# Sharing one reciprocal and one weight product among four heads in a mixture-of-softmaxes kernel, with other exponential tiles, fewer waits and an order set by hand

## The chip, the cores and the metric

One core of one Trainium2 chip. Times are device microseconds (us) of whole executions. The profiled span is about 2 us shorter than the time (781.4 for 783.36 us). A run is called fast when it lies within 1.5% of the fastest of the same kernel; all comparisons here are between fast runs.

## The reference

Shapes: logits 32 x 128 x 4 x 4096 and prior 32 x 128 x 4, fp32; output 32 x 128 x 4096.

```python
prior_probs = np.exp(prior - prior.max(axis=-1, keepdims=True))
prior_probs = prior_probs / prior_probs.sum(axis=-1, keepdims=True)
softmax = np.exp(logits - logits.max(axis=-1, keepdims=True))
softmax = softmax / softmax.sum(axis=-1, keepdims=True)
mixture = np.sum(prior_probs[..., None] * softmax, axis=2)
```

Each of the 4096 rows has four heads of 4096 logits. The kernel takes exponentials without subtracting the maximum, sums them on the way, and adds the four heads, each times prior / sum. It reads 268.5 MB and writes 67.1 MB.

## The kernel before

The work is cut into 32 units of 128 rows. A unit's load is 8.39 MB (128 rows of 64 KB), its store 2.10 MB. Two load tiles alternate; exponentials are taken on ACT (ScalarE) and go to two tiles by turns; each head gets its own reciprocal on DVE (VectorE) and, except head 0, its own product on POOL (GpSimd). SP (SyncE) issues the loads. In the cut of the code that follows, the comments are mine.

```python
for b in range(B):
    ...
    if 0 < b < B - 3:
        store(b - 1, eng=nc.scalar)          # the store of the unit before, on ACT's queue
    for h in range(H):
        ...
        et = lt[:, h] if inplace else ebuf[:, h % 2]
        ex = nc.scalar.activation(et, lt[:, h], AF.Exp, accum_out=dsum[:, col])
        ...
        nc.vector.reciprocal(rden[:, col], dsum[:, col])
        if h == 0:
            nc.vector.tensor_scalar(out=acc, in0=et, scalar1=rden[:, col], scalar2=pp[...],
                                    op0=ALU.mult, op1=ALU.mult)
            continue
        nc.gpsimd.tensor_mul(coeff[:, col], rden[:, col], pp[...])
        ...
            nc.vector.scalar_tensor_tensor(out=acc[:, cs], in0=et[:, cs], scalar=coeff[:, col],
                                           in1=acc[:, cs], op0=ALU.mult, op1=ALU.add)
            if split:                         # the very last add and its store, in two halves
                store(b, c * w, (c + 1) * w)
    if b + 2 < B:
        load(b + 2)
    if b == B - 3:                            # the last stores go behind the loads, on SP's queue
        store(b - 1)
        store(b)
    elif b == B - 2:
        store(b)
```

Loads of unit 0 and of the last three units go in four pieces of one head each. The last two units work inside the load tile.

The softmax here doesn't subtract the row's maximum and nothing guards it: scores larger than these inputs give would overflow.

## Time and profile before

| | before |
|---|---|
| time, median of the first 3 runs | 783.39 us (783.36 to 783.53) |
| profiled span | 781.4 us |
| DVE, ACT, POOL busy | 531.3, 470.4, 19.3 us |
| bytes over the span | 335.67 MB, 430 GB/s |
| DMA queues together | 99.7% of 16 engines' span |

The page lists the busy time of each engine, then 40 slices of the span, then the DMA queues. In the chain of waits, columns are start, duration, and what the step is. In tables by stretches: the stretch, its length, busy us of DVE, ACT and POOL with counts, clock, DMA share, GB/s. The DMA share books each packet at one moment, so a short stretch can read a little over 1.00. The lines that carry the argument stand in the prediction.

### The profile page before, as it was taken

Reading aid. Unit: us, or ns where it says so; the run is one execution under the profiler, and the core shown is the slowest. Engines: PE = TensorE matmul, PEld = TensorE weight load, DVE = VectorE, ACT = ScalarE, POOL = GpSimd, SP = SyncE. Lnnn points to the kernel's source line nnn. Section 1 sums busy time; section 2 is a strip of 40 time slices with the busy share of each in tenths; the row PEclk is TensorE's granted clock in tenths of the full one; section 3 lists DMA queues with packets and bytes.
Section 4 is the critical chain, followed back from the end, with each engine's and each line's share of the span. In section 5 each row is a group of like instructions: output and inputs, shape, how many; then the busy total and the mean of one; then the engine's idle time right before and its main releaser. Section 6 shows DMA issues by size and latency. Waiting matters only on the chain.

```text
span 781.4 us, 853 instructions
## 1 busy us (share of the span) xinstructions
DVE 531.3 (68%) x266; ACT 470.4 (60%) x258; POOL 19.3 (2%) x101
## 2 busy tenths in 40 slices
DVE  6647678656786666866667765677666776668994
ACT  5366556755567555576555765457655577558971
POOL 0000000000000000000000000000000000000000
DMA  9999999999999999999999999999999999999998
GB/s 377 445 416 456 416 419 453 416 457 408 461 406 466 406 463 409 426 447 424 448 413 465 404 461 405 460 420 451 411 451 418 433 439 416 456 413 429 429 429 357
DMA packets 11127, 335.67 MB, mean 430 GB/s; under 512 B 1248, under 2 KB 1248, under 8 KB 1264
## 3 DMA queue, kind: packets, MB, share of 16 engines
q1 hardware_dynamic: 7056, 276.83, 82.1%
q10 hardware_dynamic: 4064, 58.79, 17.6%
q14 instruction: 7, 0.06, 0.0%
HBM read 268.50 MB, written 67.11 MB: 429 GB/s over the span
## 4 chain that ended last, share of the span: by engine, by line
DMA 66%; ACT 14%; DVE 10%; issue 7%; SPq 0%; POOL 0%; DVEq 0%; POOLq 0%; ACTq 0%
DMA ltile<-in_logits_dram 66%; ACT ebuf L110 14%; DVE acc L131 9%; DVE ltile L131 1%; SPq L51 0%; POOL coeff L126 0%; DVE rden L119 0%; DVEq L169 0%; DVE ltile L121 0%; POOLq L169 0%; ACTq L110 0%
## 5 line engine op out<-in xcount | busy, mean ns | idle before, releaser
L110 ACT ACTIVATE ebuf<-ltile 128x4096 f32<-128x4096 f32 x120 | 433.0, 3609 | 284.1 <-DMA ltile<-in_logits_dram 240.5
L131 DVE SCALAR_TENSOR_TENSOR acc<-ebuf,coeff,acc 128x4096 f32<-128x4096 f32 x90 | 403.6, 4484 | 27.3 <-POOL coeff L126 27.3
L119 DVE RECIPROCAL rden<-dsum 128x1 f32<-128x1 f32 x128 | 20.4, 159 | 203.8 <-ACT ebuf L110 203.8
L121 DVE TENSOR_SCALAR acc<-ebuf,rden,pp 128x4096 f32<-128x4096 f32 x30 | 72.4, 2412 | 1.1
L126 POOL TENSOR_TENSOR coeff<-rden,pp 128x1 f32<-128x1 f32 x96 | 18.2, 189 | 747.1 <-DVE rden L119 747.1
L110 ACT ACTIVATE ltile<-ltile 128x4096 f32<-128x4096 f32 x8 | 28.9, 3608 | 4.3 <-DMA ltile<-in_logits_dram 4.3
L131 DVE SCALAR_TENSOR_TENSOR ltile<-ltile,coeff 128x4096 f32<-128x4096 f32 (+1 forms) x7 | 27.0, 3874 | 1.8 <-POOL coeff L126 1.8
L110 ACT ACTIVATION_READ_ACCUMULATOR ebuf<-ltile 128x1 f32 x120 | 22.4, 187 | 0.0
L121 DVE TENSOR_SCALAR ltile<-ltile,rden,pp 128x4096 f32<-128x4096 f32 x2 | 4.8, 2414 | 0.1
L68 DVE TENSOR_REDUCE pmax<-pr 16x256 f32<-16x1024 f32 x1 | 1.2, 1207 | 4.8 <-DMA pr<-in_prior_dram 4.8
L70 ACT ACTIVATE pr<-pr 16x1024 f32<-16x1024 f32 x1 | 1.1, 1055 | 4.9 <-DVE pr L69 4.9
L70 ACT ACT_TABLE_LOAD x1 | 1.3, 1283 | 1.2 <-PEq L158 1.2
L73 DVE TENSOR_TENSOR pn<-pr,pmax 16x1024 f32<-16x1024 f32 x1 | 1.9, 1906 | 0.1
L71 DVE TENSOR_REDUCE pmax<-pr 16x256 f32<-16x1024 f32 x1 | 1.2, 1207 | 1.1 <-ACT pr L70 1.1
L80 DVE STREAM_TRANSPOSE pp<-pn 32x256 f32<-32x256 f32 x4 | 1.7, 434 | 0.1
L72 DVE RECIPROCAL pmax<-pmax 16x256 f32<-16x256 f32 x1 | 1.7, 1741 | 0.0
L110 ACT ACTIVATION_READ_ACCUMULATOR ltile<-ltile 128x1 f32 x8 | 1.5, 186 | 0.0
L69 DVE TENSOR_TENSOR pr<-pr,pmax 16x1024 f32<-16x1024 f32 x1 | 1.2, 1214 | 0.0
L66 POOL MEMSET pn<- 32x1024 f32 x1 | 0.9, 941 | 0.3 <-POOLq L158 0.3
L158 POOL MEMSET const-float32-0.0<- 128x1 f32 x1 | 0.1, 103 | 0.2 <-issue 0.2
L158 POOL MEMSET const-bfloat16-1.0<- 128x1 bf16 x1 | 0.1, 106 | 0.0
L158 POOL MEMSET const-uint8-127<- 128x1 uint8 x1 | 0.1, 106 | 0.0
(1 smaller groups left out, 0.1 us busy)
## 6 DMA issues: line engine op xcount, KB each, us to landing
out_dram<-acc ACTq DMA_DIRECT2D x28, 2048.0 KB, 29.3
ltile<-in_logits_dram SPq DMA_DIRECT2D x16, 2048.0 KB, 20.4
out_dram<-acc SPq DMA_DIRECT2D x2, 2048.0 KB, 32.9
out_dram<-ltile SPq DMA_DIRECT2D x1, 2048.0 KB, 21.2
out_dram<-ltile SPq DMA_DIRECT2D x2, 1024.0 KB, 8.7
ltile<-in_logits_dram SPq DMA_DIRECT2D x28, 32.3
pr<-in_prior_dram ACTq DMA_DIRECT2D x1, 64.0 KB, 4.1
```

The lines of the kernel that those rows point to most:

```text
L68: nc.vector.reduce_max(pmax, pr, axis=AX.X)
L69: nc.vector.tensor_sub(pr, pr, pmax.unsqueeze(2).to_broadcast([G, R, H]))
L70: nc.scalar.activation(pr, pr, AF.Exp)
L71: nc.vector.reduce_sum(pmax, pr, axis=AX.X)
L72: nc.vector.reciprocal(pmax, pmax)
L73: nc.vector.tensor_mul(pn[0:G].rearrange("g h r -> g r h"), pr, pmax.unsqueeze(2).to_broadcast([G, R, H]))
L80: nc.vector.transpose(pp[32 * t : 32 * (t + 1)], pq[:, :, :, 32 * t : 32 * (t + 1)])
L110: ex = nc.scalar.activation(et, lt[:, h], AF.Exp, accum_out=dsum[:, col])
L119: nc.vector.reciprocal(rden[:, col], dsum[:, col])
L121: nc.vector.tensor_scalar(out=acc, in0=et, scalar1=rden[:, col], scalar2=pp[:, b % J, h, b // J : b // J + 1], op0=ALU.mult, op1=ALU.mult,)
L126: nc.gpsimd.tensor_mul(coeff[:, col], rden[:, col], pp[:, b % J, h, b // J : b // J + 1])
L131: nc.vector.scalar_tensor_tensor(out=acc[:, cs], in0=et[:, cs], scalar=coeff[:, col], in1=acc[:, cs], op0=ALU.mult, op1=ALU.add,)
```

## The change

The intent: take work and waits from DVE, ACT and POOL. One reciprocal of four columns and one product of four columns serve all heads of a unit. Head 0's exponential is written over its own logits, heads 1 and 3 go to SBUF tiles, head 2 to PSUM, so that ACT need not wait for a tile that DVE still reads. Each instruction keeps only the waits named for it, and the order of the program is that of the source. In exchange the adds of a unit wait for its fourth exponential, the next load into the tile waits for the first add, and the store goes out later.

```diff
-            et = lt[:, h] if inplace else ebuf[:, h % 2]
-            ex = nc.scalar.activation(et, lt[:, h], AF.Exp, accum_out=dsum[:, col])
-            nc.vector.reciprocal(rden[:, col], dsum[:, col])
-            nc.gpsimd.tensor_mul(coeff[:, col], rden[:, col], pp[...])
+    ebuf1 = cpool.tile([P, V], FP32, name="ebuf1")
+    ebuf2 = psum.tile([P, V], FP32, name="ebuf2")
+    ebuf3 = cpool.tile([P, V], FP32, name="ebuf3")
+            byhead = u >= U - 3
+            es = (lt[:, 0], ebuf1, ebuf2, ebuf3) if bufd else [lt[:, h] for h in range(H)]
...
+            if not byhead:
+                for h in range(H - 1):
+                    exp(h)
+                if u:
+                    store(u - 1, obuf[:, (u - 1) % 2], nc.scalar)
+                exp(H - 1, ...)
+                mul = weigh(0, H, *free)      # one reciprocal, one product, 128x4
+                for h in range(H):
+                    add(h, mul)
+            else:                              # the last three units: head by head as before
+                for h in range(H):
+                    exp(h)
+                    mul = weigh(h, 1, ...)
+                    ...
...
+            if u >= 2:                         # in load(u)
+                only(ld, adds[u - 2, 0] if h == 0 else exps[u - 2, h])
```

(`only` keeps the waits that are named and drops the others; parts of the diff are left out, and the comments are mine.)

More of the change, by code (lines that the diff above doesn't have):

```diff
@@ L29 @@
     G = B * S // R
-    B = G * J
-    assert G * R == B * S and G <= 32
+    U = G * J
+    assert G * R == B * S and G <= 32 and H == 4
     lg = logits.rearrange("b s h v -> (b s) h v").rearrange("(g p j) h v -> g j p h v", p=P, j=J)
@@ L35 @@
     pv = prior.rearrange("b s h -> (b s) h").rearrange("(g r) h -> g r h", r=R)
-    lpool = ctx.enter_context(tc.tile_pool(name="lpool", bufs=2))
-    apool = ctx.enter_context(tc.tile_pool(name="apool", bufs=2))
     cpool = ctx.enter_context(tc.tile_pool(name="cpool", bufs=1))
-    def pieces(b):
-        return 1 if b == 0 or b >= B - 3 else H
-    ltiles = {}
-    def load(b, eng=nc.sync):
-        lt = lpool.tile([P, H, V], FP32, name="ltile")
-        n = pieces(b)
-        for h in range(0, H, n):
-            eng.dma_start(out=lt[:, h : h + n], in_=lg[b // J, b % J, :, h : h + n, :])
-        ltiles[b] = lt
@@ L54, with only @@
-    accs = {}
-    def store(b, lo=0, hi=V, eng=nc.sync):
-        eng.dma_start(out=ov[b // J, b % J, :, lo:hi], in_=accs[b][:, lo:hi])
-    load(0, eng=nc.sync)
+    psum = ctx.enter_context(tc.tile_pool(name="psum", bufs=1, space=bass.MemoryType.PSUM))
+    before = {}
+    def only(ins, *keep):
+        for k in keep:
+            tc.add_manual_dep(
+                ins.ins,
+                k.ins.name,
+                mybir.DependencyInfo(mybir.DependencyClass.Sync, mybir.DependencyReason.DATA),
+                reason="all that this instruction waits for",
+            )
+        tc.declare_no_dep(
+            ins.ins,
+            group="loop",
+            keep=[k.ins for k in keep] + before.get(ins.ins.engine, []),
+            reason="covered by the waits that are kept",
+        )
+        tc.add_to_no_dep_group("loop", ins.ins)
+        before[ins.ins.engine] = [ins.ins]
+        return ins
@@ new lines, with load @@
+    ltile = cpool.tile([P, 2, H, V], FP32, name="ltile")
+    loads = {}
+    exps = {}
+    adds = {}
+    stores = {}
+    def load(u):
+        n = 1 if u == 0 or u >= U - 3 else H
+        for h in range(0, H, n):
+            ld = nc.sync.dma_start(
+                out=ltile[:, u % 2, h : h + n], in_=lg[u // J, u % J, :, h : h + n, :]
+            )
+            if u >= 2:
+                only(ld, adds[u - 2, 0] if h == 0 else exps[u - 2, h])
+            else:
+                only(ld)
+            for k in range(h, h + n):
+                loads[u, k] = ld
@@ L62, with store @@
+    def store(u, acc, eng, lo=0, hi=V):
+        st = eng.dma_start(out=ov[u // J, u % J, :, lo:hi], in_=acc[:, lo:hi])
+        stores[u] = only(st, adds[u, H - 1])
     pr = cpool.tile([G, R, H], FP32, name="pr")
-    nc.scalar.dma_start(out=pr, in_=pv)
-    load(1, eng=nc.sync)
     pn = cpool.tile([32, H, R], FP32, name="pn")
-    nc.gpsimd.memset(pn, 0.0)
     pmax = cpool.tile([G, R], FP32, name="pmax")
-    nc.vector.reduce_max(pmax, pr, axis=AX.X)
-    nc.vector.tensor_sub(pr, pr, pmax.unsqueeze(2).to_broadcast([G, R, H]))
@@ L70 @@
-    nc.scalar.activation(pr, pr, AF.Exp)
-    nc.vector.reduce_sum(pmax, pr, axis=AX.X)
-    nc.vector.reciprocal(pmax, pmax)
-    nc.vector.tensor_mul(
-        pn[0:G].rearrange("g h r -> g r h"), pr, pmax.unsqueeze(2).to_broadcast([G, R, H])
-    )
-    pq = pn.rearrange("g h (p j) -> g j h p", j=J)
-    pp = cpool.tile([P, J, H, 32], FP32, name="pp")
-    for t in range(P // 32):
-        nc.vector.transpose(pp[32 * t : 32 * (t + 1)], pq[:, :, :, 32 * t : 32 * (t + 1)])
-    NCHUNK = 2
-    dsum = cpool.tile([P, B * H], FP32, name="dsum")
@@ L86 @@
-    rden = cpool.tile([P, B * H], FP32, name="rden")
-    coeff = cpool.tile([P, B * H], FP32, name="coeff")
-    ebuf = cpool.tile([P, 2, V], FP32, name="ebuf")
-    exps = []
-    for b in range(B):
-        last = b == B - 1
-        inplace = b >= B - 2
-        lt = ltiles.pop(b)
-        if not inplace:
-            accs[b] = apool.tile([P, V], FP32, name="acc")
-        else:
-            accs[b] = lt[:, 0]
-        acc = accs[b]
-        if 0 < b < B - 3:
-            store(b - 1, eng=nc.scalar)
-        for h in range(H):
-            split = last and h == H - 1
-            i = b * H + h
-            col = slice(i, i + 1)
-            et = lt[:, h] if inplace else ebuf[:, h % 2]
-            ex = nc.scalar.activation(et, lt[:, h], AF.Exp, accum_out=dsum[:, col])
-            if h == 0:
-                tc.keep_in_program_order(ex)
-            if not inplace:
-                if len(exps) >= 2:
-                    tc.declare_no_dep(ex.ins, exps[-2], reason="covered by the sum")
-                exps.append(ex.ins)
-            nc.vector.reciprocal(rden[:, col], dsum[:, col])
-            if h == 0:
-                nc.vector.tensor_scalar(
-                    out=acc, in0=et, scalar1=rden[:, col], scalar2=pp[:, b % J, h, b // J : b // J + 1],
-                    op0=ALU.mult, op1=ALU.mult,
-                )
-                continue
-            nc.gpsimd.tensor_mul(coeff[:, col], rden[:, col], pp[:, b % J, h, b // J : b // J + 1])
-            n = NCHUNK if split else 1
-            w = V // n
-            for c in range(n):
-                cs = slice(c * w, (c + 1) * w)
-                nc.vector.scalar_tensor_tensor(
-                    out=acc[:, cs], in0=et[:, cs], scalar=coeff[:, col], in1=acc[:, cs],
-                    op0=ALU.mult, op1=ALU.add,
-                )
-                if split:
-                    store(b, c * w, (c + 1) * w)
-        if b + 2 < B:
-            load(b + 2)
-        if b == B - 3:
-            store(b - 1)
-            store(b)
-        elif b == B - 2:
-            store(b)
@@ new lines, with exp, weigh, add @@
+    pp = cpool.tile([P, J, H, 32], FP32, name="pp")
+    dsum = cpool.tile([P, U, H], FP32, name="dsum")
+    rden = cpool.tile([P, U, H], FP32, name="rden")
+    coeff = cpool.tile([P, U, H], FP32, name="coeff")
+    ebuf1 = cpool.tile([P, V], FP32, name="ebuf1")
+    ebuf2 = psum.tile([P, V], FP32, name="ebuf2")
+    ebuf3 = cpool.tile([P, V], FP32, name="ebuf3")
+    obuf = cpool.tile([P, 2, V], FP32, name="obuf")
+    with tc.manual_schedule():
+        load(0)
+        nc.scalar.dma_start(out=pr, in_=pv)
+        load(1)
+        nc.gpsimd.memset(pn, 0.0)
+        nc.vector.reduce_max(pmax, pr, axis=AX.X)
+        nc.vector.tensor_sub(pr, pr, pmax.unsqueeze(2).to_broadcast([G, R, H]))
+        nc.scalar.activation(pr, pr, AF.Exp)
+        nc.vector.reduce_sum(pmax, pr, axis=AX.X)
+        nc.vector.reciprocal(pmax, pmax)
+        nc.vector.tensor_mul(
+            pn[0:G].rearrange("g h r -> g r h"), pr, pmax.unsqueeze(2).to_broadcast([G, R, H])
+        )
+        pq = pn.rearrange("g h (p j) -> g j h p", j=J)
+        for t in range(P // 32):
+            nc.vector.transpose(pp[32 * t : 32 * (t + 1)], pq[:, :, :, 32 * t : 32 * (t + 1)])
+        for u in range(U):
+            bufd = u < U - 2
+            byhead = u >= U - 3
+            lt = ltile[:, u % 2]
+            acc = obuf[:, u % 2] if bufd else lt[:, 0]
+            es = (lt[:, 0], ebuf1, ebuf2, ebuf3) if bufd else [lt[:, h] for h in range(H)]
+            ppu = pp[:, u % J, :, u // J]
+            def exp(h, *keep):
+                ex = nc.scalar.activation(
+                    es[h], lt[:, h], AF.Exp, accum_out=dsum[:, u, h : h + 1]
+                )
+                keep = (loads[u, h],) + keep
+                if bufd and h and u:
+                    keep += (adds[u - 1, h],)
+                exps[u, h] = only(ex, *keep)
+            def weigh(h, n, *keep):
+                rc = nc.vector.reciprocal(rden[:, u, h : h + n], dsum[:, u, h : h + n])
+                only(rc, exps[u, h + n - 1])
+                mul = nc.gpsimd.tensor_mul(
+                    coeff[:, u, h : h + n], rden[:, u, h : h + n], ppu[:, h : h + n]
+                )
+                return only(mul, rc, *keep)
+            def add(h, mul, lo=0, hi=V):
+                if h == 0:
+                    st = nc.vector.tensor_scalar(
+                        out=acc[:, lo:hi], in0=es[h][:, lo:hi], scalar1=coeff[:, u, h : h + 1],
+                        scalar2=None, op0=ALU.mult,
+                    )
+                    adds[u, h] = only(st, mul)
+                else:
+                    st = nc.vector.scalar_tensor_tensor(
+                        out=acc[:, lo:hi], in0=es[h][:, lo:hi], scalar=coeff[:, u, h : h + 1],
+                        in1=acc[:, lo:hi], op0=ALU.mult, op1=ALU.add,
+                    )
+                    adds[u, h] = only(st, mul, adds[u, h - 1])
+            free = (stores[u - 2],) if bufd and u >= 2 else ()
+            if not byhead:
[3 more added lines that the diff above has]
+                    store(u - 1, obuf[:, (u - 1) % 2], nc.scalar)
+                exp(H - 1, *((stores[u - 4],) if u >= 4 else ()))
+                mul = weigh(0, H, *free)
+                for h in range(H):
+                    add(h, mul)
+            else:
+                for h in range(H):
+                    exp(h)
+                    mul = weigh(h, 1, *(free if h == 0 else ()))
+                    n = 2 if u == U - 1 and h == H - 1 else 1
+                    w = V // n
+                    for c in range(n):
+                        add(h, mul, c * w, (c + 1) * w)
+                        if n > 1:
+                            store(u, acc, nc.sync, c * w, (c + 1) * w)
+            if u + 2 < U:
+                load(u + 2)
+            if u == U - 3:
+                store(u - 1, obuf[:, (u - 1) % 2], nc.sync)
+                store(u, acc, nc.sync)
+            elif u == U - 2:
+                store(u, acc, nc.sync)
```

## The prediction

> **What bounds the kernel now.** I read the page from the top down: busy shares, the 40 slices, the queues. Then the table by stretches, the chain in order of time, and the timeline of one middle unit and of the last 90 us. A unit is 128 rows of 4 heads: an 8.39 MB load and a 2.10 MB store. There are 32, numbered 0 to 31.
>
> The page:
>
> ```profile
> span 781.4 us, 853 instructions
> ...
> DVE 531.3 (68%) x266; ACT 470.4 (60%) x258; POOL 19.3 (2%) x101
> ...
> DMA  9999999999999999999999999999999999999998
> ...
> DMA packets 11127, 335.67 MB, mean 430 GB/s; under 512 B 1248, under 2 KB 1248, under 8 KB 1264
> ...
> q1 hardware_dynamic: 7056, 276.83, 82.1%
> q10 hardware_dynamic: 4064, 58.79, 17.6%
> ```
>
> No engine is near full, while the two DMA queues together take 82.1 + 17.6 = 99.7% of the 16 DMA engines. Queue q1 carries the loads, q10 the stores that ACT issues. Two stretches of two units each, and the end, from the table by stretches (DVE, ACT, POOL busy, clock, DMA share, GB/s):
>
> ```profile
> 236.53:284.85 48.32, 32.68 (x16) 29.24 (x17) 1.14 (x6) 1.00 1.00 434
> 284.85:333.18 48.33, 32.68 (x16) 29.23 (x17) 1.14 (x6) 1.00 1.00 434
> ```
>
> ```profile
> 765.00:770.00 5.00, 4.70 (x4) 0.00 (x0) 0.19 (x1) 1.00 0.98 419
> 770.00:775.00 5.00, 1.62 (x1) 0.00 (x0) 0.00 (x0) 1.00 0.99 423
> 775.00:782.00 7.00, 0.00 (x0) 0.00 (x0) 0.00 (x0) 1.00 0.49 206
> ```
>
> Two units are 20.97 MB; in 48.33 us that is 434 GB/s, or 24.17 us a unit. DMA stays full until 775 + 0.49 x 7 = 778.4, so only the first 2 us and the last 3 are without transfers. The chain of waits, in order of time:
>
> ```profile
> 284.85 7.32 ACT ebuf L110 x4
> ...
> 297.20 3.50 issue
> 300.70 0.19 ACT ebuf L110
> 300.91 32.25 DMA ltile<-in_logits_dram
> 333.18 7.32 ACT ebuf L110 x4
> ```
>
> It reads as if exponentials and load alternated in a loop of 48.3 us. But a load alone needs 8.39 MB / 434 GB/s = 19.3 us: the 32.25 us are mostly standing in line behind the load before it. What the loop leaves spare: unit 11 is whole at 284.85, its successor's successor is issued at 300.91, 16.1 us later, and the engines need it only 24.2 us after 284.85, less 2 to 3 us to start and land. So 5 to 6 us are to spare. A change on ACT or DVE that keeps the load's issue inside them moves nothing.
>
> At the end another thing bounds almost as tightly. DVE from the timeline of the last 90 us:
>
> ```profile
> 700.76 2.41 DVE L121 TENSOR_SCALAR acc<-ebuf,rden,pp 128x4096 f32<-128x4096 f32 x1
> ...
> 718.94 2.41 DVE L121 TENSOR_SCALAR acc<-ebuf,rden,pp 128x4096 f32<-128x4096 f32 x1
> ...
> 737.40 2.41 DVE L121 TENSOR_SCALAR ltile<-ltile,rden,pp 128x4096 f32<-128x4096 f32 x1
> ...
> 754.50 2.42 DVE L121 TENSOR_SCALAR ltile<-ltile,rden,pp 128x4096 f32<-128x4096 f32 x1
> ...
> 767.01 4.61 DVE L131 SCALAR_TENSOR_TENSOR ltile<-ltile,coeff 128x2048 f32<-128x2048 f32 x2 [0.30 <-POOL coeff L126]
> ```
>
> Units 28 to 31 start at 700.76, 718.94, 737.40 and 754.50, some 17 to 18 us apart, and DVE ends at 771.6. Here units no longer arrive 24 us apart for DVE: it works without a pause from unit 28 on, because loads run ahead of the last stores. It still ends before DMA has drained.
>
> [...]load packets of 64 KB beside store packets of 16 KB give 82 to 18%, and from 693 to 703 us, where loads come in 16 KB packets, the DMA view has 49.4 to 41.3%; a store takes 13.3 us there instead of the median 29.3. [...] No run of the kernel before touches PSUM.
>
> **The change, part by part.** T is when a unit has landed whole; middle units only, unless said.
>
> Reciprocals and weights: 29 units lose 3 of 4 reciprocals (0.16 us, group list) and have one POOL product for four where they had three. That takes 87 x 0.16 = 14 us of busy time from DVE, and three waits of 0.30 us a unit from between its adds. All of it beside the DMA: worth 0 in the middle. The price: the one reciprocal waits for the fourth exponential.
>
> Exponentials: four tiles instead of two, so ACT no longer waits 1.42 us for DVE before head 3. Head spacing 3.61 us (309.01, 312.62, 316.22 in the timeline), so the fourth sum is there at T + 14.5; reciprocal, product and start of the first add follow at +0.2, +0.24 and +0.23 in the old timeline: adds begin at T + 15.0. Before it was 312.95 - 309.01 = 3.9. They take 2.41 + 3 x 4.49 + gaps = 16.0, end T + 31.0. The next unit's exponentials of heads 1 to 3, at T + 24.2 + 3.6, 7.2, 10.8, find heads 1 to 3 added at T + 22.0, 26.5, 31.0: no wait.
>
> The load two units on now waits for the first add, because head 0 is exponentiated inside the load tile: T + 17.5 instead of T + 16.1. It spends 1.4 of the spare 5 to 6 us: no DMA gap, 0 us.
>
> The store moves from T + 22 (306.89 - 284.85) to after the next unit's third exponential was dispatched, T + 24.2 + 7.3 to 11: 10 to 13 us later. Total bytes stay. With 24.2 us beside a load plus about 3 to start and land, it lands about 10 to 14 us into the unit that reuses the buffer, which asks for it at 14.6. Close, but if it is late, stores are queued meanwhile, so the DMA engines have work.
>
> Start: all four heads of unit 0 must be in before the first add (27.5 instead of 15.3), load 2 goes out near 30 instead of 27.0; loads 0 and 1 keep the queue full to about 41. 0 us.
>
> End: the only place where I find a cost. The stores' delay lets unit 28 land about 2.3 us earlier (11 us of a 20% share): 696.8 becomes 694.5. Unit 28 still shares its reciprocal, so DVE starts it at T + 15.0, not at +3.9, and leaves it at T + 31.0. Store 27, which unit 29 waits for, goes at the 16 KB rate and lands by T + 24: no wait. Units 29 to 31 go head by head as before, with POOL now also ahead of head 0 (+0.37): 2.79 + 3 x 4.86 = 17.4 us each, from the spacings 740.18, 745.04, 749.91. DVE ends at T + 31.0 + 52.2 + 0.1 for the split = T + 83.3, near 777.8 instead of 771.6: 6.2 us later. DMA, by the old backlog, has stored unit 30 by T + 79.0; the first half of the last store is issued at T + 81.1 and moves from 82.3; the second ends at 87.2. So DMA idles 3.3 us. The old end adds 2.9 us (781.4 - 778.5): T + 90.1 = 784.6 us.
>
> Sum: middle 0, start 0, end +3.2: span 784.6, and with the 2.0 us by which the time exceeds the span (783.39 - 781.4), 786.6 us.
>
> **The rivals.** First, nothing moves: 783.4, give or take 0.5. For it: DMA at 99.7%, same bytes and packets. It holds if the last units' DVE work is hidden: if DVE's lateness is 3 us less than I sum, or the stores lag further than I think. Second, the buffer wait takes the place of what was removed: if stores need 33.5 us (the longest of the 28 in the view of the store line) instead of 27 to 29, the product waits, the load behind the first add goes out past T + 21, and the load queue runs dry for 1 us or so in many units. Thirty times 0.3 to 0.5 us would make 796 to 802. Against it: the landing store is itself DMA work, and the next store is already queued, so it corrects itself; engines run in step, with clean 3 us beats of packets. Third, compute was the limit and the freed DVE and ACT time pays: 14 us less DVE, 43.5 us less ACT waiting would give up to 765. [...]I give it almost nothing.
>
> **Range and chances.** 786.6 us, 8 in 10 from 782.8 to 791. Below lies rival one; above, a little of rival two. Faster by 2% means under 767.7[...]: 0.01. Slower by 2% needs 15.7 us of DMA idleness, only rival two in force: 0.04. Within: 0.95.
>
> **What would show it.** Right: middle stretches still 48.3 us at 434 GB/s; ACT's wait for DVE gone; issue to landing of middle loads about 1 to 2 us shorter; stores longer or equal; DVE busy near 517; a first add 15 us after a unit lands; at the end DVE running unbroken to about 778, and a hole of about 3 us in DMA before the last stores. Wrong: no hole (rival one), or POOL waiting for stores and DMA shares below 0.98 in the middle (rival two). [...]

(At the 434 GB/s of the middle stretches the 335.67 MB take 773.4 us. The 2 to 3 us "to start and land" were an estimate; in experiments 5 and 6 a load that was issued late took 27.0 us, 2.8 more than the 24.2 us of a unit.)

## More of the kernel before

One line of the page that the prediction passed over turns out to matter, the third DMA queue of the kernel before (packets, MB, share):

```profile
q14 instruction: 7, 0.06, 0.0%
```

By its kind this queue carries the engines' own programs: seven pieces of 8192 bytes and 0.31 to 0.32 us each. They pass over the same DMA engines: while one is under way, 15 data packets are in flight in the trace, where there are 16 just before and after.

## The result

The changed kernel took 784.08 us, median of 6 runs (783.99 to 784.74), beside 783.44 us of the kernel before, 6 runs (783.31 to 783.93). The ratio is 1.0009, 95% interval 0.9996 to 1.0022: no verdict of faster or slower, though the two sets of runs do not overlap. A ratio is the mean time of one kernel's fast runs over that of the other's fast runs of the same rounds, so it is not quite the ratio of the medians quoted. The time lies inside the range that was predicted. The forecast of a loss of 3.2 us was too large: it is 0.6 us.

The page of the changed kernel:

```profile
span 782.2 us, 680 instructions
...
DVE 520.9 (67%) x179; ACT 467.4 (60%) x258; POOL 9.3 (1%) x46
...
q1 hardware_dynamic: 7056, 276.83, 82.0%
q10 hardware_dynamic: 4064, 58.79, 17.6%
q14 instruction: 5, 0.04, 0.0%
```

DVE and POOL lost 10 us of busy time each and the program 173 instructions; the two data queues carry the same packets and still fill the DMA engines. Who waited for whom, first in the kernel before, then in the changed one (us in total, times, longest):

```profile
ACT ebuf L110 <- DVE acc L131: 43.5, 31, 1.4
```

```profile
ACT ebuf L132 <- DVE obuf L156: 5.5, 3, 3.8
```

ACT's waits for DVE went from 43.5 to 5.5 us, as meant. The middle, by stretches of two units, and the chain of waits there:

```profile
258.81:307.16 48.35, 31.97 (x11) 29.02 (x17) 0.40 (x2) 1.00 1.00 434
307.16:355.50 48.34, 31.96 (x11) 29.01 (x16) 0.40 (x2) 1.00 1.00 434
```

```profile
307.16 3.71 ACT ltile L132 x2
...
322.19 2.36 DVE obuf L150
324.57 30.91 DMA ltile<-in_logits_dram
```

Two units still take 48.35 us at 434 GB/s. The first add begins 322.19 - 307.16 = 15.0 us after the unit landed, the load two units on is issued at +17.4 us, and it lands 30.91 us later where it took 32.25: what it is issued later, it stands less in line. The middle won and lost nothing.

The end, DVE in the timeline of the last 140 us:

```profile
709.12 2.35 DVE L150 TENSOR_SCALAR obuf<-ltile,coeff 128x4096 f32<-128x4096 f32 x1 [0.32 <-POOL coeff L143]
...
725.41 2.35 DVE L150 TENSOR_SCALAR obuf<-ltile,coeff 128x4096 f32<-128x4096 f32 x1 [0.30 <-POOL coeff L143]
...
760.04 2.35 DVE L150 TENSOR_SCALAR ltile<-ltile,coeff 128x4096 f32<-128x4096 f32 x1 [0.31 <-POOL coeff L143]
...
772.50 4.61 DVE L156 SCALAR_TENSOR_TENSOR ltile<-ltile,coeff 128x2048 f32<-128x2048 f32 x2 [0.31 <-POOL coeff L143]
```

Unit 28 starts at 709.12 where it started at 700.76, and DVE ends at 777.1 instead of 771.6. What DMA did meanwhile, in stretches of 2 us, the kernel before and then the changed kernel:

```profile
776.00:778.00 2.00, 0.00 (x0) 0.00 (x0) 0.00 (x0) 1.00 1.02 434
778.00:780.00 2.00, 0.00 (x0) 0.00 (x0) 0.00 (x0) 1.00 0.19 78
```

```profile
772.00:774.00 2.00, 1.69 (x3) 0.00 (x0) 0.19 (x1) 1.00 0.48 205
774.00:776.00 2.00, 2.00 (x2) 0.00 (x0) 0.00 (x0) 1.00 0.16 66
776.00:778.00 2.00, 1.11 (x1) 0.00 (x0) 0.00 (x0) 1.00 1.05 430
778.00:780.00 2.00, 0.00 (x0) 0.00 (x0) 0.00 (x0) 1.00 1.01 422
780.00:782.00 2.00, 0.00 (x0) 0.00 (x0) 0.00 (x0) 1.00 0.32 131
```

The predicted hole is there: 2 x 0.52 + 2 x 0.84 = 2.7 us of missing transfers between 772 and 776. But look at how the two kernels finish. Before, the rate falls to a fifth at 778, and the last packet came after 780: the DMA share falls from 1.02 to 0.19, the share of 3 of 16 engines, so most had finished at 778 and a few ran on for 2 us. The changed kernel, after its hole, moves at full rate (1.05 and 1.01) to about 780.6 and stops at once: its last 16 packets of data end between 780.72 and 780.89.

Finer stretches show where the stragglers went, first the end of the kernel before, then the hole of the changed one:

```profile
778.60:779.60 1.00, 0.00 (x0) 0.00 (x0) 0.00 (x0) 1.00 0.17 74
```

```profile
773.00:774.20 1.20, 1.20 (x1) 0.00 (x0) 0.00 (x0) 1.00 0.17 68
774.20:775.60 1.40, 1.40 (x2) 0.00 (x0) 0.00 (x0) 1.00 0.00 0
```

A share of 0.17 is about 3 of 16 engines (3 packets are in flight at 779.0). In the hole a few transfers go on until 774.1 us, then for 1.6 us there is none at all, and at 775.7 all 16 engines begin together (16 packets start between 775.71 and 775.86). (The trace does not name the engine of a packet; I count packets in flight.) The last data packet ends at 780.1 us in the kernel before and at 780.9 in the changed one, 1.3 us before the end of the span in both.

### The profile page after: what moved, and what is told of

Same layout as the page of the kernel before. It is cut to its first block, busy times and chain, and to the rows that moved or that the text cites. A ratio compares the mean times of both kernels' runs of the same rounds, so it can differ in the third digit from the quotient of the medians.

```text
span 782.2 us, 680 instructions
## 1 busy us (share of the span) xinstructions
DVE 520.9 (67%) x179; ACT 467.4 (60%) x258; POOL 9.3 (1%) x46
## 3 DMA queue, kind: packets, MB, share of 16 engines
q1 hardware_dynamic: 7056, 276.83, 82.0%
q10 hardware_dynamic: 4064, 58.79, 17.6%
## 4 chain that ended last, share of the span: by engine, by line
DMA 59%; ACT 26%; DVE 12%; issue 1%; POOL 1%; DVEq 0%; SPq 0%; POOLq 0%
DMA ltile<-in_logits_dram 59%; ACT ebuf L132 20%; ACT ltile L132 6%; DVE obuf L150 5%; DVE obuf L156 3%; DVE ltile L156 3%; POOL coeff L143 1%; DVE ltile L150 1%; DVE rden L141 0%; DVEq L214 0%; SPq L72 0%; POOLq L214 0%
## 5 line engine op out<-in xcount | busy, mean ns | idle before, releaser
L156 DVE SCALAR_TENSOR_TENSOR obuf<-ebuf,coeff,obuf 128x4096 f32<-128x4096 f32 x90 | 403.6, 4484 | 4.0 <-POOL coeff L143 0.9
L132 ACT ACTIVATE ebuf<-ltile 128x4096 f32<-128x4096 f32 x90 | 323.0, 3589 | 9.0 <-DVE obuf L156 5.5
L132 ACT ACTIVATE ltile<-ltile 128x4096 f32<-128x4096 f32 x38 | 137.4, 3615 | 281.3 <-DMA ltile<-in_logits_dram 281.2
L141 DVE RECIPROCAL rden<-dsum 128x4 f32<-128x4 f32 (+1 forms) x41 | 7.0, 171 | 234.1 <-ACT ebuf L132 234.1
L150 DVE TENSOR_SCALAR obuf<-ltile,coeff 128x4096 f32<-128x4096 f32 x30 | 70.6, 2353 | 9.5 <-POOL coeff L143 9.5
L143 POOL TENSOR_TENSOR coeff<-rden,pp 128x4 f32<-128x4 f32 (+1 forms) x41 | 8.2, 199 | 762.6 <-DVE rden L141 762.6
L132 ACT ACTIVATION_READ_ACCUMULATOR ebuf<-ltile 128x1 f32 x90 | 16.8, 186 | 0.0
L132 ACT ACTIVATION_READ_ACCUMULATOR ltile<-ltile 128x1 f32 x38 | 7.1, 186 | 0.0
L150 DVE TENSOR_SCALAR ltile<-ltile,coeff 128x4096 f32<-128x4096 f32 x2 | 4.7, 2354 | 0.6 <-POOL coeff L143 0.6
## 6 DMA issues: line engine op xcount, KB each, us to landing
out_dram<-ltile SPq DMA_DIRECT2D x1, 2048.0 KB, 14.8
ltile<-in_logits_dram SPq DMA_DIRECT2D x28, 30.9
```

The costliest lines, as they stand in the source:

```text
L132: ex = nc.scalar.activation(es[h], lt[:, h], AF.Exp, accum_out=dsum[:, u, h : h + 1])
L141: rc = nc.vector.reciprocal(rden[:, u, h : h + n], dsum[:, u, h : h + n])
L143: mul = nc.gpsimd.tensor_mul(coeff[:, u, h : h + n], rden[:, u, h : h + n], ppu[:, h : h + n])
L150: st = nc.vector.tensor_scalar(out=acc[:, lo:hi], in0=es[h][:, lo:hi], scalar1=coeff[:, u, h : h + 1], scalar2=None, op0=ALU.mult,)
L156: st = nc.vector.scalar_tensor_tensor(out=acc[:, lo:hi], in0=es[h][:, lo:hi], scalar=coeff[:, u, h : h + 1], in1=acc[:, lo:hi], op0=ALU.mu ...
```

## The experiments

**Theory A.** The middle costs nothing. The loss is the hole at the end, made by DVE starting unit 28 late; part of it is given back because in the hole the engines that lag behind catch up. **Theory B.** The 0.6 us come from the middle: later loads, later stores, other tiles. **Theory C**, added to A: DMA engines lag because instruction fetches land on them (0.31 us each, as above), and the changed kernel has fewer (5 instead of 7). "Before" is each time the kernel before on the same chip; the first four runs shared nine runs of it, 783.38 us (783.31 to 783.82), the next four eleven, 783.42 us (783.24 to 783.62), the last three nine, 783.47 us (783.31 to 783.63). The changed kernel was not run again on these chips; its 784.08 us stand beside 783.44 of the kernel before, which these chips give within 0.06 us.

### 1. Unit 28 head by head

```diff
-            byhead = u >= U - 3
+            byhead = u >= U - 4
 ...
                     exp(h)
+                    if u == U - 4 and h == 1:
+                        store(u - 1, obuf[:, (u - 1) % 2], nc.scalar)
```

> The changed kernel with unit 28 (the fourth from the end) also weighed head by head, so that DVE starts it about 8 us sooner after landing. Theory A (the changed kernel loses only at its end: DVE is late, DMA runs dry for some 3 us before the last store, and part of this is given back because the old kernel's DMA engines finish unevenly): DVE ends near 771 instead of 777, no hole in DMA before the last store, the uneven end of the old kernel returns, time 783.4 +- 0.3, that is 0.7 us below the changed kernel. Theory B (the 0.6 us come from the middle, from the later loads and stores): the hole goes but the time stays at 784.1.

Measured: 782.77 us (782.58 to 783.50, 5 runs), ratio 0.9992 to the kernel before, interval 0.9980 to 1.0005. DVE ended at 770.5. The end by stretches:

```profile
776.00:778.00 2.00, 0.00 (x0) 0.00 (x0) 0.00 (x0) 1.00 0.95 401
778.00:780.00 2.00, 0.00 (x0) 0.00 (x0) 0.00 (x0) 1.00 0.10 41
```

The hole is gone, and with it 1.3 us against the changed kernel: the hole made the loss, and theory B falls, since nothing in the middle was altered. The return to 783.4 did not come; it is 0.6 us below that. DMA again is full to 778, but the last data packet now came near 779 and not after 780. Both this and the changed kernel fetched 5 pieces of instructions until then, the kernel before 7.

### 2. The last store in quarters, in the changed kernel

```diff
-                    n = 2 if u == U - 1 and h == H - 1 else 1
+                    n = 4 if u == U - 1 and h == H - 1 else 1
```

> The changed kernel with the last add and its store in four pieces instead of two. Theory A: the hole before the last store is what sets the end, and the first piece goes out 1.2 us sooner, so the time falls by about 1.2 us to 782.9, below both kernels. Theory B (the end is set by the bytes that DMA has to move, not by DVE): no change, 784.1.

Measured: 783.16 us (783.07 to 784.89), 0.9 us below the changed kernel by the medians; the ratio to the kernel before is 1.0002 (0.9989 to 1.0014), so it is not shown to be below both kernels. The profiled span fell from 782.2 to 781.1 us. Most of what theory A expected; not all of the 1.2 us came.

### 3. The same in the kernel before

```diff
-    NCHUNK = 2
+    NCHUNK = 4
```

> The same edit in the kernel before, where DMA never runs dry before the last store. Theory A: nothing to win, 783.4 +- 0.2. If the wait from the end of DVE to the end of the store set the end there as well, it would fall by about 1.2 us to 782.2.

Measured: 783.10 us (782.89 to 783.18), 0.28 us below before, so just outside the 0.2 that was allowed for. Where there is no hole, the finer split gains a quarter of a us and not 1.2.

### 4. Every unit head by head

```diff
-            byhead = u >= U - 3
+            byhead = True
 ...
             else:
+                if 0 < u < U - 3:
+                    store(u - 1, obuf[:, (u - 1) % 2], nc.scalar)
 ...
-                only(ld, adds[u - 2, 0] if h == 0 else exps[u - 2, h])
+                only(ld, *((adds[u - 2, 0], exps[u - 2, n - 1]) if h == 0 else (exps[u - 2, h],)))
```

(The third edit keeps the load safe: the first add no longer comes after all four exponentials.)

> The changed kernel with every unit weighed head by head (one reciprocal and one product a head) and with the store issued ahead of the exponentials as in the kernel before; the PSUM tile, the load tile, the kept waits and the order by hand stay. Theory A: the sharing and the late store are what delays DVE at the end, so without them 783.4 +- 0.3, DVE ending near 771 and no hole. Theory B (the tiles, the waits or the order cost the 0.6 us): 784.1.

Measured: 783.23 us (783.13 to 783.39), 0.15 us below before. No hole, DVE done at 770.9, DMA full to 778, last data packet near 780; 6 fetches. The tiles in PSUM and in the load tile, the trimmed waits and the order by hand, taken together without the sharing and the late store, cost nothing that shows.

### 5 and 6. Loads issued later still

This tests the spare time of a load that the prediction put at 5 to 6 us after 16.1 us.

```diff
-                only(ld, adds[u - 2, 0] if h == 0 else exps[u - 2, h])
+                only(ld, adds[u - 2, 1] if h == 0 and n == H else adds[u - 2, 0] if h == 0 else exps[u - 2, h])
```

(The second run has `adds[u - 2, 3]` in place of `adds[u - 2, 1]`.)

> The changed kernel with every middle load issued after the second add of its buffer's unit instead of the first: about 22.0 us after that unit landed instead of 17.5. Theory A (a middle load has 5 to 6 us to spare over the 16.1 us of the kernel before, and stores fill what gap there is): 784.1 +- 0.5, issue to landing of a middle load 4.5 us shorter (about 26.4). Rival (exponentials and load form a loop, as the chain of waits reads, so each us of delay is paid once in two units): 15 x 4.5 = +67 us, 851.

> The same after the fourth add, about 31.0 us after landing, that is some 9 us beyond the spare time. Theory A: the load queue runs dry for about 9 us in each unit, stores fill at most 4.8 us of it, so 2 to 4.5 us are lost a unit and the time becomes 845 to 915. Rival (a loop with no spare time): 15 x 13.5 = +203 us, 987.

Measured: 796.76 us after the second add (fast runs 794.98 to 798.65; a sixth, 832.30, was slow), 915.14 us after the fourth (914.86 to 916.95). The chains of waits, first run and second:

```profile
431.29 4.50 DVE obuf L156
435.81 27.01 DMA ltile<-in_logits_dram
```

```profile
445.46 4.50 DVE obuf L156
449.98 26.98 DMA ltile<-in_logits_dram
```

In these two runs a load that is issued late needs 27.0 us to land, whether after the second or the fourth add (in the chains, leaving out the first one or two, 26.9 to 28.0). In the unchanged schedules it shows 32.3 or 30.9; I take the rest for the line ahead of it. So two units take the larger of 48.35 us and issue + 27.0. At +17.4 that is 44.4: hidden, 3.9 us to spare. The edit reaches 27 loads, 13.5 pairs. At +22.0 it is 49.0: 0.65 us too much for each pair, 13.5 x 0.65 = 8.8 us, of the 12.7 us measured against the changed kernel. The rest is in the same place: in the profiled run (798.65 us) loads took up to 28.0 us in the first 300 us, and two units then 49.2 to 50.0. From unit 2 to unit 28 it needs 641.6 us where the changed kernel needs 627.2, that is 14.4 of the 14.6 us by which this run is longer. Why those loads took longer stays open. At +31.0 it is 58.0: 13.5 x 9.65 = 130 us; 131 were measured. My first expectation of "784.1 +- 0.5" failed because 22.0 is just beyond the limit of 48.35 - 27.0 = 21.35, which 5 to 6 us of spare time did not resolve. The loop without spare time (851 and 987) failed by far more.

### 7 and 8. More instructions to fetch, first try

```diff
+    scrap = cpool.tile([P, 1], FP32, name="scrap")
 ...
+        for _ in range(20):
+            nc.gpsimd.memset(scrap, 0.0)
```

> The kernel before with 20 one-column memsets of an unused tile on the idle POOL in each unit, 640 in all, which nothing waits for. Theory C (instructions are fetched over the same DMA engines in pieces of 8 KB, seen as the instruction queue; each piece sets back the one engine that carries it by some 0.3 us, and the end of the kernel waits for the engine that is furthest behind): about 5 more fetches[...], DMA full to about 778 as before but its uneven end longer than 780.3, time +0.5 to +1.5 us. Rival (the uneven end comes from the data transfers themselves): 41 KB are 0.1 us of all engines, time unchanged within 0.2.

> The same with 60 memsets a unit, 1920 in all, about 15 more fetches. Theory C: about three times what 640 of them cost, +1 to +4 us. Rival: within 0.3 us of the kernel before.

Measured: 818.92 us and 921.45 us. Far above both theories, and for another reason. The waits of the first:

```profile
DVE acc L132 <- POOL scrap L139: 40.1, 4, 29.3
```

DVE stood up to 29.3 us behind the memsets. The order of the kernel before is the scheduler's: it set memsets of many units in a row at the front of POOL's program, and products had to wait for them. The two runs say nothing on fetches. They do show what an unconstrained scheduler may do with work that nothing depends on.

### 9 and 10. The same with the order by hand

```diff
             ...                       # unit 28 by head, after the last product of each unit:
+            for _ in range(20):
+                nc.gpsimd.memset(scrap, 0.0)
             if u + 2 < U:
                 load(u + 2)
```

> The fetch question again, without the fault of the last try (there the scheduler put the memsets of many units at the front of POOL's program, where products had to wait for them): the kernel with unit 28 by head, whose order is by hand, with 20 memsets of an unused column after the last product of each unit, 2.1 us in POOL's 24 us pause. Theory C: about 5 more instruction fetches, each sets one DMA engine back, middle stretches of two units that hold one last 0.2 to 0.6 us longer, the uneven end grows; time +0.3 to +1.5 us over 782.77. Rival (fetches cost nothing): 782.8 +- 0.2.

> The same with 60 a unit, 6.3 us in POOL's pause, about 15 more fetches. Theory C: +1 to +4 us over 782.77. Rival: 782.8 +- 0.3.

Measured with 20 a unit: 785.10 us (784.97 to 785.26), 2.3 us above the same kernel without them. It fetched 10 pieces of instructions until 779 us, where the kernel of experiment 1 fetched 5. Three stretches of two units; the second holds the only fetch of these:

```profile
300.64:348.96 48.32, 31.96 (x10) 29.01 (x16) 8.39 (x43) 1.00 1.00 434
348.96:397.96 49.00, 31.96 (x10) 29.01 (x16) 8.38 (x43) 1.00 0.99 430
397.96:446.31 48.35, 31.96 (x10) 29.01 (x16) 8.38 (x43) 1.00 1.00 434
```

The memsets themselves cost nothing: the first and third stretch have 40 of them and are as short as ever. The stretch with the fetch is 0.65 us longer. And the end:

```profile
778.00:780.00 2.00, 0.00 (x0) 0.00 (x0) 0.00 (x0) 1.00 0.20 82
780.00:782.00 2.00, 0.00 (x0) 0.00 (x0) 0.00 (x0) 1.00 0.05 20
```

DMA as a whole is done at 778 as in the kernel before; a few transfers go on, from 779.5 us only one at a time, until 781.7. DVE ended at 772.2 and not at 770.5, because unit 28 landed 1.7 us later (696.1 instead of 694.4); DMA is full until then, so there is no hole. Theory C holds in kind; in size I had said +0.3 to +1.5 us, and it is 2.3 for five fetches, 0.46 us each on average. Single fetches differ: around the one at 148.7 us two units took 48.49, only 0.14 us more than without a fetch.

With 60 a unit: 805.08 us (802.15 to 808.73), where I had said +1 to +4. It made 20 fetches, and early stretches that hold one are 49.0 us long again, later ones up to 50.8, which one fetch each does not explain. And here POOL itself was late at the end (DVE waited three times 4.9 us for products there), and DMA stood empty before the last stores (no packet from 792.5 to 798.4 us). So this run mixes two causes; I take only its direction.

### 11. The version that beats both

Experiment 1 and the quarters of experiment 2 together.

> Unit 28 by head together with the last store in four pieces, the version that should beat both kernels. No hole before the last store, so the pieces win no more than the 0.3 us that they won in the kernel before: 782.5 +- 0.3, DMA full to about 778.

Measured: 782.56 us (782.28 to 783.82, 5 runs), ratio 0.9991, interval 0.9977 to 1.0004. Four of its five runs lie below every run of either kernel; in size it is 0.9 us of 783 and inside the interval of no difference.

## Why the prediction was right or wrong

**The middle: right.** Adds at +15.0, load at +17.4, no ACT waits, 48.35 us for two units at 434 GB/s, all as worked out. Experiments 5 and 6 put the spare time at 5.25 us after +16.1 (4.3 where a load took 28.0), where 5 to 6 was said. What was not seen is how sharply it ends.

**The buffer wait (rival two): did not happen.** POOL waited for no store in the changed kernel: in the middle a store landed 12.0 us after the unit that reuses its buffer (657.8 for a unit landed at 645.8; said 10 to 14), and was asked for at 14.8. The third rival, freed compute time, brought nothing either.

**DVE's lateness at the end: right.** Unit 28 landed at 694.1 (said 694.5), DVE ended at 777.1 (said 777.8). The mechanism, four heads behind one reciprocal and then three units without a pause, is as predicted, and experiment 1 shows that it makes the loss. The landing itself was partly luck: the prediction put all of the 2.3 us by which unit 28 comes sooner down to the later stores. It came 2.7 us sooner, but only 1.4 of them were there at unit 4 (113.6 instead of 114.9; 115.0 in experiment 4, whose stores are early again). The other 1.4 arose between units 4 and 28, which lie 581.9 us apart in the kernel before and 580.5 in the changed one; the fetches come into that below.

**The size of the loss: wrong, at the last step of the sum.** The prediction said "So DMA idles 3.3 us. The old end adds 2.9 us (781.4 - 778.5)". The hole was 2.7 us, 0.6 less. The 2.9 us were taken for a fixed time after the last transfer. They are not: some 1.7 of them in the kernel before (778.4 to 780.1, at a DMA share of 0.17) were a few engines that ran on after the others, and only the 1.3 us after the last packet are the same in both. In the hole the stragglers were done by 774.1, all engines started together, and from 780.6 only 782.2 - 780.6 = 1.6 us remained, 1.3 less than 2.9. So 3.2 - 0.6 - 1.3 leaves 1.3 us for the hole. The hole is thus paid for to a good part with idleness that the old kernel had anyway, at its very end. With the same 5 fetches, hole or no hole is 784.08 to 782.77: 1.3 us, not 3.3.

**A term that was left out.** The changed kernel has 173 fewer instructions and 5 fetches instead of 7. At the 0.46 us of experiment 9 that is 0.9 us by estimate, a rough one: around the fetch at 350.0 us in the kernel before two units took 48.37 us, that is nothing more, around those at 471.6 and 487.0 they took 49.35, and around the changed kernel's fetch at 511.8 they took 48.56. Measured are 0.6 us, between the kernel before and experiment 1. So +1.3 for the hole and -0.6 for the rest give the +0.6 to +0.7 that was seen. That fetches delay is shown by experiment 9; that they are the whole difference between experiment 1 and the kernel before is only consistent with the runs (5 fetches 782.8 us, 6 fetches 783.2, 7 fetches 783.4, 10 fetches 785.1), as these kernels differ in other things too. Why a stretch grows by more than the 0.31 us of a piece, why trailing engines have not caught up by the end, and why one fetch costs more than another, the runs do not show.

**Also off:** the start of the last store's transfer after its issue (1.2 us said, 0.8 seen), and DVE's busy time (517 said, 520.9 seen). One reading in the prediction was loose without consequence: the 82 to 18% of the two queues are simply the bytes of the whole run (276.83 and 58.79 MB); that the queues share by packets is seen only in the stretch from 693 to 703 us (from 697 on, with packets of 16 KB in both, 79 of loads and 76 of stores). Of PSUM the runs show this: the 90 fused adds of the changed kernel, a third of them from PSUM, took 4483 to 4486 ns all, as did the 90 of the kernel before, all from SBUF; the changed kernel's exponentials of head 2, written to PSUM, took 3562 to 3588 ns, those of heads 1 and 3, written to SBUF, 3598 to 3617.

## What to carry to other kernels

Where transfers filled the DMA engines (99.7% of the span), work taken from the other engines (10 us from DVE, 10 from POOL) was worth nothing in the middle: two units took 48.33 us before and 48.35 after. In such a kernel look instead at what the new order does to the last few units, where the pace of arrival no longer hid compute here: 17 to 18 us from unit to unit on DVE instead of 24.2. Keep the batch form for the middle and go back to item by item early enough before the end. And do not add a hole in a saturated resource to the old end in full: first ask how much of the old end was already idleness of single engines (1.7 of 2.9 us here), and count what the change does to program length (five more fetches went with 2.3 us in experiment 9).
